# A 256-row attention trunk in fp32r on one core: plain rows for the weight parts, and products in four passes of sixteen groups of eight columns

## The chip, the cores and the metric

The kernel runs on one core of a Trainium2 chip. Its engines work side by side, each through its own list of instructions in order: TensorE (PE) multiplies, VectorE (DVE) and ScalarE (ACT) do the arithmetic on tiles, GpSimd (POOL) and SyncE (SP) mostly issue DMAs. The weight loads of TensorE are told apart as PEld. The metric is the device time in microseconds, the median of several runs. Fp32r is the 32-bit type in which the products are made; a number is given to them as the sum of two fp32r parts, a high and a low one.

## The reference

x has 256 rows of 4096 columns; there are 32 heads of 128, and only layer 0 runs (DEPTH is 1). Cut to what matters:

```python
h = x + attn_branch(rms_norm(x, norm_attn), w_in_attn, w_out_attn)
return rms_norm(h, final_norm)

def attn_branch(xn, w_in, w_out):            # w_in 4096 x 16384, w_out 4096 x 4096
    q, k, v, g = jnp.split(xn @ w_in, 4, axis=-1)
    o = stick_breaking_attention(to_heads(q), to_heads(k), to_heads(v))
    return (o * jax.nn.silu(g)) @ w_out

# per head, for s < t:  z = q.k / sqrt(128)
# log_a[t, s] = log_sigmoid(z_ts) + sum over s < j < t of log_sigmoid(-z_tj);   o_t = sum_s exp(log_a) v_s
```

Nearly all of the work is in the two big products, x times w_in and o times w_out.

## The kernel before

The products are cut into 20 units of 512 x 2 output columns: 16 for w_in (two heads each, with their q, k, v and gate) and 4 for w_out. Each unit goes through 16 steps of 256 rows of the weights. In the first unit of each matrix a step is eight products of 128 x 128 by 128 x 512. In the other units ten of the sixteen steps use a scheme with seven products in place of eight (sums and differences of weight blocks, and of blocks of x, stand for the blocks), the other six steps eight. The outputs of a unit collect in seven accumulators in PSUM (`acc`, the rings `b1` to `b7`) and are combined at the unit's end.

A weight block arrives by a DMA from SP into a `raw` tile; for the steps with seven products GpSimd adds another block on top by a second DMA. VectorE makes the further sums inside `raw` (`sums`, lines 411 to 432). Then `piece` (line 438) splits the block: ScalarE writes the high part `wh`, a copy rounded to fp32r, and VectorE the low part `wl`, the block minus `wh`. A part holds two 512-column operands (c = 0 and 1), each made of two halves of 256 columns (i = 0 and 1). Parts of only one operand lie in a smaller tile, of which one half serves as `wh` and the other as `wl`; in the trace both bear the name wh. Of x, and later of the attention's output, the stationary operands are split in the same way: `sh` and `sl` for x, `oh` and `ol` for the output (the `forms`).

`mm3` (line 797) is one product: three matmuls, high by high, high by low and low by high, into one accumulator. `mm3` is called for the big products only; the attention's matmuls (tiles tr, z and o, and neg_tri for the scan along the keys) are written out by themselves, read plain rows, and write plain rows.

In the kernel before, `by_runs` (line 434) lays the 1024 columns of a part in runs of four: sixteen columns in a row hold four of (c 0, i 0), four of (c 0, i 1), four of (c 1, i 0), four of (c 1, i 1), and so on. A product reads its operand in two passes, one for each half: 64 runs of four columns, each run sixteen columns (64 bytes) after the one before. The accumulator is written in one plain row.

The order of the instructions comes from `Plan` (line 108), which runs through the program as a simulation of its own while the program is being written out, with a cost for each instruction, and gives every engine the waiting work with the lowest key. The products' order is fixed (`order`, line 301); their cost is `PRODUCT`, three times `tensor_ns(512)`, and the keys of the other work are multiples of it. Where the attention's work, the splits and the sums fall between the products thus hangs on `tensor_ns` (line 104). `SPREAD` (line 58) says from which step on the forms of the attention's output are made for w_out: form s may start when step 12 + s, counted from the start of the last unit of w_in, is done (`later_than`, line 941). The number of buffers (7 for raw, 7 for wh, 5 for wl) limits how far the splits run ahead of the products.

Of the kernel before, what the change touches and what calls it, by code (L numbers as in the profile page):

```python
# [11 lines left out]
F32R = mybir.dt.float32r  # L12
# [7 lines left out]
P = 128  # L20
# [6 lines left out]
HG = CW // P  # L27
NB = D // CW
W = 2 * CW
NJ = D // W  # L30
KT = 2
NS = KC // KT
EPS = 1e-6

RUN = 4
WARM, IDLE = 10, 640


# [9 lines left out]
LOWS = 5  # L48
# [6 lines left out]
KEPT = 5  # L55
LAST_ORDER = (5, 4, 2, 3)

SPREAD = (12, 1.0)
HEADS_AHEAD = 0
SUMS_LATER = 2  # L60
H_LATER = 6
# [40 lines left out]


def tensor_ns(n):
    return 0.4167 * n + 12.4 if n > 128 else 109.0


class Plan:
# [135 lines left out]
def kernel(  # L244
# [14 lines left out]
    wp = ctx.enter_context(tc.tile_pool(name="weights", bufs=1))  # L259
# [10 lines left out]
    def minus(out_, full, part):  # L270
        nc.vector.tensor_tensor(out=out_, in0=full, in1=part.bitcast(F32), op=ALU.subtract)
# [30 lines left out]
    for b in LAST_ORDER:  # L302
        order += [(n, k) for n in kept for k, prod in enumerate(parts[n]["prods"]) if prod[0] == b]
    starts, ends, first, left, place_of = {}, {}, {}, {}, {}
    PRODUCT = 3 * tensor_ns(W)
    for g, (n, k) in enumerate(order):
        p = parts[n]
# [17 lines left out]
    def dve(emit, n, key=None, more=0, **kw):  # L325
        n = n if isinstance(n, tuple) else (n,)
        cost = sum(vector_ns(m) for m in n) + 122 * (len(n) - 1) + more
        return nc.work("vector", cost, emit, soon() if key is None else key, **kw)

    def act(emit, n, key=None, **kw):  # L330
        n = n if isinstance(n, tuple) else (n,)
        cost = sum(scalar_ns(m) for m in n) + 100 * (len(n) - 1)
        return nc.work("scalar", cost, emit, soon() if key is None else key, **kw)
# [4 lines left out]
    def ten(emit, *n):  # L338
        return nc.work("tensor", 40 + sum(tensor_ns(m) for m in n), emit, nc.here - 1e4, wait=400)
# [20 lines left out]
    raw, wh, wl = {}, {}, {}  # L360
# [44 lines left out]
    def low_done(n):  # L405
        lows_left[n] -= 1
        if not lows_left[n]:
            nc.tell(("lows", n))
            tile_done(*parts[n]["tile"])

    def sums(q):

        a, b, c, d = quad_parts[q]
        one, two = raw[q, 0], raw[q, 1]
        for k in range(2):
            tile_left[q, k] += 1

        def add(to, at_, f, g, key, op=ALU.add):
            return dve(
                lambda: nc.vector.tensor_tensor(out=to[:, :, at_, :], in0=f, in1=g, op=op), W,  # L420
                key - SUMS_AHEAD * 1e3, more=120 if op == ALU.subtract else 10,
            )

        yield nc.until(("lows", a), ("T3", q))
        yield add(one, 0, one[:, :, 0, :], two[:, :, 0, :], first[c], ALU.subtract)
        yield nc.until(("lows", b))
        yield add(two, 1, one[:, :, 0, :], two[:, :, 1, :], first[c])
        nc.tell(("sums", c))
        yield add(one, 1, one[:, :, 0, :], one[:, :, 1, :], first[d])
        nc.tell(("sums", d))  # L430
        for k in range(2):
            tile_done(q, k)

    def by_runs(t):

        return t.rearrange("p (h c i e) -> p c i h e", c=KT, i=HG, e=RUN)

    def piece(n, c, there):

        p = parts[n]  # L440
        yield nc.until(*there)
        full = raw[p["tile"]][:, :, p["place"], :][:, :, c, :].rearrange("p i c (h e) -> p c i h e", e=RUN)
        h = wh[n][:, c]
        size = (c.stop - c.start) * W
        key = first[n] - (AHEAD * 1e3 if p["seven"] and p["i"] < 2 else 0)
        yield act(lambda: nc.scalar.copy(h, full), size, key - 2.0 * 1e3)
        if p["size"] == KT:
            if c.start == 0:
                yield nc.take("wl")
                wl[n] = by_runs(wp.tile([P, KT * W], F32R, tag="wl", name=f"wl{n}", bufs=LOWS))  # L450
                nc.tell(("lowslot", n))
            else:
                yield nc.until(("lowslot", n))
        l = wl[n][:, c]
        if n == 0:
            yield nc.until(("sh", c.start))
        yield dve(lambda: minus(l, full, h), size, key, more=10)
        for k in range(c.start, c.stop):
            nc.tell(("low", n, k))
        low_done(n)  # L460

    def split(size, tag, bufs):
        for n, p in enumerate(parts):
            if p["size"] != size:
                continue
            q = p["quad"]
            t = p["tile"][1]
            if size == KT:
                yield nc.take(tag)
            yield nc.until(("raw", q, t))  # L470
            if size < KT:
                yield nc.take(tag)
            wh[n] = by_runs(wp.tile([P, KT * W], F32R, tag="wh" if size == KT else "s", name=f"wh{n}", bufs=bufs))
            if size == 1:
                wh[n], wl[n] = wh[n][:, 0:1], wh[n][:, 1:2]
            cuts = [slice(k, k + 1) for k in range(KT)] if n == 0 else [slice(0, size)]
            lows_left[n] = len(cuts)
            if p["seven"] and p["i"] == 0:
                nc.start(sums(q))
            for c in cuts:  # L480
                nc.start(piece(n, c, [("sums", n)] if p["seven"] and p["i"] > 1 else [("raw", q, t)]))
# [315 lines left out]
    def mm3(out_, a, b, start, stop):  # L797

        (ah, al), (bh, bl) = a, b
        if len(bh.shape) == 4:  # L800
            out_ = out_.rearrange("p (i h e) -> p i h e", i=HG, e=RUN)
        kw = dict(skip_group_check=True)
        nc.tensor.matmul(out_, ah, bh, start=start, stop=False, **kw)
        nc.tensor.matmul(out_, ah, bl, start=False, stop=False, **kw)
        nc.tensor.matmul(out_, al, bh, start=False, stop=stop, **kw)
# [135 lines left out]
    def later_than(u, s):  # L941
        s = int(SPREAD[0] + SPREAD[1] * s)
        return "used", u + s // NS, s % NS
# [284 lines left out]
    def product(n, k):  # L1228
        p = parts[n]
        b, f, c = p["prods"][k]  # L1230
        h, l = forms[p["s"]]
        mm3(
            ev[p["u"]][b],
            (h[:, PLACES[f], :], l[:, PLACES[f], :]),
            (wh[n][:, c], wl[n][:, c]),
            starts[p["u"], b] == (n, k),
            ends[p["u"], b] == (n, k),
        )

    def products():  # L1240
        for g, (n, k) in enumerate(order):
            p = parts[n]
            u, s = p["u"], p["s"]
            b, f, c = p["prods"][k]
            if u < 1:
                what = "s"
            elif u < OUT0:
                what = "n"
            elif u == OUT0:
                what = "o"  # L1250
            else:
                what = "r" if u == LAST and s in EIGHT_LAST else "p"
            if starts[u, b] == (n, k):
                yield nc.take(f"b{b}")
                ev.setdefault(u, {})[b] = acc.tile([P, W], F32, tag=f"b{b}", name=f"acc{u}_{b}")
            yield nc.until(("low", n, c), ("form", what, s), lead=nc.LEAD)
            yield nc.work(
                "tensor", PRODUCT, lambda: product(n, k), g * PRODUCT, after=lambda n=n, k=k: done(n, k), hold=False
            )
            nc.here = g * PRODUCT  # L1260

    together(split(KT, "w", HIGHS), split(1, "s", SINGLES), products(), x_stats(), x_factor(), constants())

    def in_turn(works):
# [55 lines left out]
```

## Time and profile before

| what | us |
|---|---|
| median of three runs (1722.3 to 1724.72) | 1723.66 |
| the profiled execution | 1725.08 |
| its span, first to last instruction | 1722.3 |
| TensorE busy in it | 1704.4 |
| VectorE busy in it | 1634.9 |
| ScalarE busy in it | 1199.3 |
| HBM read, 403.98 MB | 239 GB/s over the span |

A row of a group reads: line, engine, operation, tile written and tiles read, shape and count, then busy time in us, mean of one in ns, and idle time ahead of it with what ended that. Nearly every row has line 127, the planner's helper that emits all instructions; so groups are told apart by their tiles. A matmul lasts longer than the time to the next one's start, since they are pipelined. A row of windows reads: stretch, then for each engine busy us and count of instructions, the granted clock of TensorE, the DMAs' share and GB/s; of the engines the order is PE, PEld, DVE, ACT, POOL, and where one tile and engine were asked for, there is only one such pair. A row of waits reads: who waited for whom, us in total, times, longest. Where a row of a tile has three numbers after its count, they are the shortest, median and longest duration in ns.

### The profile page before, as it was taken

The page shows a single profiled execution, that of the slowest core. Times are in us where ns is not written, and L with a number is a line of the kernel's source. Part 1 is how long each engine was busy: PE and PEld are TensorE (multiplying, and loading weights), DVE is VectorE, ACT ScalarE, POOL GpSimd, SP SyncE. Part 2 cuts the span into 40 slices and gives each one's busy share as a digit, 9 for nine tenths or more (in the row PEclk, how much of TensorE's full clock was granted, in tenths as well). Part 3 has the DMA queues.
Part 4 walks back from the last instruction along what each step waited for, and adds up shares of the span by engine and source line. Part 5 has one row for each costly group of instructions (what it writes and reads, how often), then busy time and mean ns, then how long its engine had stood idle before and what let it go on. Part 6 is the DMA issues. An engine that isn't in the chain of part 4 may idle for free. (4 is left out here: it accounts for less than half of the span.)

```text
span 1722.3 us, 25298 instructions
## 1 busy us (share of the span) xinstructions
PE 1704.4 (99%) x7735; PEld 1415.7 (82%) x7735; DVE 1634.9 (95%) x2106; ACT 1199.3 (70%) x1640; POOL 335.6 (19%) x407
## 2 busy tenths in 40 slices
PE   9999999999999999999999999999999999999997
PEld 7888888888888888888888888888888888878786
DVE  8899999999999999999999999999999978999997
ACT  8986767676767676767676767676767765666655
POOL 0012222222222222121212121212222112122120
PEclk9999999999999999999999999999999999999999
DMA  9978787878787979797978787878788978898895
GB/s 342 329 199 234 220 248 221 247 215 259 206 264 197 266 194 273 191 270 199 266 202 257 207 249 216 245 214 245 221 238 224 278 243 253 232 258 248 242 301 196
DMA packets 249384, 413.82 MB, mean 240 GB/s; under 512 B 28128, under 2 KB 73440, under 8 KB 249248
## 3 DMA queue, kind: packets, MB, share of 16 engines
q1 hardware_dynamic: 194544, 354.24, 62.2%
q0 software_dynamic: 54416, 57.70, 20.4%
q8 instruction: 60, 0.98, 0.2%
q14 instruction: 76, 0.62, 0.1%
q10 hardware_dynamic: 288, 0.28, 0.0%
HBM read 403.98 MB, written 8.13 MB: 239 GB/s over the span
## 5 line engine op out<-in xcount | busy, mean ns | idle before, releaser
L127 ACT CAST wh<-raw 128x1024 fp32r<-128x1024 f32 (+1 forms) x995 | 922.3, 969 | 412.2 <-DVE raw L127 207.3
L127 DVE TENSOR_TENSOR wl<-raw,wh 128x1024 fp32r<-128x1024 f32 (+1 forms) x818 | 974.9, 1218 | 33.7 <-PE acc L127 13.5
L127 PE MATMUL acc<-wh,sh 128*128 128x512 f32 x2048 | 783.5, 394 | 1.1 <-DVE qk_sb L127 0.7
L127 PE MATMUL acc<-wh,sl 128*128 128x512 f32 x1898 | 733.3, 386 | 0.0
L127 PE MATMUL acc<-wl,sh 128*128 128x512 f32 x1748 | 675.3, 386 | 0.0
L127 POOL DMA_DIRECT2D raw<-in_w_in_dram x300 | 263.1, 996 | 977.8 <-DMA raw<-in_w_in_dram 326.5
L127 PEld LDWEIGHTS acc<-wh,sh 128*128 128x128 f32 x2048 | 384.1, 188 | 77.9 <-issue 2.2
L127 PEld LDWEIGHTS acc<-wh,sl 128*128 128x128 f32 x1898 | 356.1, 188 | 73.4 <-DVE sl L127 0.5
L127 PEld LDWEIGHTS acc<-wl,sh 128*128 128x128 f32 x1748 | 328.5, 188 | 61.5 <-DVE wl L127 0.4
L127 DVE TENSOR_TENSOR raw<-raw,raw 128x512 f32<-128x512 f32 x354 | 242.6, 685 | 12.8 <-DMA raw<-in_w_in_dram 9.7
L127 PE MATMUL acc<-wh,oh 128*128 128x512 f32 x512 | 194.5, 388 | 0.0
L127 PE MATMUL acc<-wh,ol 128*128 128x512 f32 x485 | 187.1, 386 | 0.0
L127 PE MATMUL acc<-wl,oh 128*128 128x512 f32 x458 | 177.4, 387 | 3.8 <-DVE wl L127 3.8
L127 DVE TENSOR_TENSOR wh<-raw,wh 128x512 fp32r<-128x512 f32 x177 | 121.2, 684 | 1.3 <-ACT wh L127 1.3
L127 DVE TENSOR_TENSOR raw<-raw 128x512 f32<-128x512 f32 x177 | 121.0, 683 | 0.0
L127 PEld LDWEIGHTS acc<-wh,oh 128*128 128x128 f32 x512 | 96.0, 188 | 19.5 <-ACT wh L127 0.4
L127 PEld LDWEIGHTS acc<-wh,ol 128*128 128x128 f32 x485 | 90.9, 187 | 18.4
L127 PEld LDWEIGHTS acc<-wl,oh 128*128 128x128 f32 x458 | 85.8, 187 | 23.3 <-DVE wl L127 6.6
L127 POOL DMA_DIRECT2D raw<-in_w_out_dram x54 | 47.3, 976 | 182.1 <-DMA raw<-in_w_out_dram 65.9
L127 ACT ACTIVATE f<-f 128x384 f32<-128x384 f32 x96 | 50.5, 526 | 3.0
L127 ACT CAST oh<-p 128x512 fp32r<-128x512 f32 (+3 forms) x46 | 20.8, 467 | 23.5 <-DVE p L127 16.7
L127 POOL DMA_DIRECT2D p<-spill x28 | 17.0, 682 | 85.3 <-ACT gl L127 26.8
(83 smaller groups left out, 781.8 us busy)
## 6 DMA issues: line engine op xcount, KB each, us to landing
raw<-in_w_in_dram SPq DMA_DIRECT2D x1024, 256.0 KB, 4.5
raw<-in_w_out_dram SPq DMA_DIRECT2D x256, 256.0 KB, 4.4
raw<-in_w_in_dram POOLq DMA_DIRECT2D x300, 128.0 KB, 5.2
p<-spill POOLq DMA_DIRECT2D x28, 256.0 KB, 4.8
raw<-in_w_out_dram POOLq DMA_DIRECT2D x54, 128.0 KB, 5.3
xr<-in_x_dram SPq DMA_DIRECT2D x16, 256.0 KB, 5.4
xres<-in_x_dram SPq DMA_DIRECT2D x16, 256.0 KB, 6.2
out_dram<-h SPq DMA_DIRECT2D x16, 256.0 KB, 2.8
```

The lines of the kernel that those rows point to most:

```text
L127: return self.tc.keep_in_program_order(getattr(self.engine, name)(*args, **kw))
```

## The change

A part now lies in plain rows: its 1024 columns are c 0 with both halves one after the other, then c 1. ScalarE and VectorE write it so. `mm3` rearranges the operand and the accumulator alike, in four passes: pass q reads columns 8q to 8q + 7 of each 32, that is sixteen groups of eight columns, each group 32 columns (128 bytes) after the one before; it writes the accumulator's columns of the same numbers. So the accumulator holds what it held before, at the same places, and is filled in another order. Beside this the planner's cost of a matmul of 512 columns falls from 225.75 to 221.85 ns, and the forms of the attention's output may start two steps sooner.

```diff
-RUN = 4
+RUN, ROUNDS = 8, 4
...
-SPREAD = (12, 1.0)
+SPREAD = (10, 1.0)
...
 def tensor_ns(n):
-    return 0.4167 * n + 12.4 if n > 128 else 109.0
+    return 0.4167 * n + 8.5 if n > 128 else 109.0
...
-    def by_runs(t):
-
-        return t.rearrange("p (h c i e) -> p c i h e", c=KT, i=HG, e=RUN)
+    def halves(t):
+
+        return t.rearrange("p (c i n) -> p c i n", c=KT, i=HG)
...
-        full = raw[p["tile"]][:, :, p["place"], :][:, :, c, :].rearrange("p i c (h e) -> p c i h e", e=RUN)
+        full = raw[p["tile"]][:, :, p["place"], :][:, :, c, :].rearrange("p i c n -> p c i n")
...
-                wl[n] = by_runs(wp.tile([P, KT * W], F32R, tag="wl", name=f"wl{n}", bufs=LOWS))
+                wl[n] = halves(wp.tile([P, KT * W], F32R, tag="wl", name=f"wl{n}", bufs=LOWS))
...
-            wh[n] = by_runs(wp.tile([P, KT * W], F32R, tag="wh" if size == KT else "s", name=f"wh{n}", bufs=bufs))
+            wh[n] = halves(wp.tile([P, KT * W], F32R, tag="wh" if size == KT else "s", name=f"wh{n}", bufs=bufs))
...
     def mm3(out_, a, b, start, stop):
         (ah, al), (bh, bl) = a, b
-        if len(bh.shape) == 4:
-            out_ = out_.rearrange("p (i h e) -> p i h e", i=HG, e=RUN)
+        in_rounds = lambda t: t.rearrange("p (h q e) -> p q h e", q=ROUNDS, e=RUN)
+        out_, bh, bl = (in_rounds(t) for t in (out_, bh, bl))
...
-            (wh[n][:, c], wl[n][:, c]),
+            tuple(t[:, c].rearrange("p i n -> p (i n)") for t in (wh[n], wl[n])),
```

The first products in TensorE's row, before and after (the number behind a tile's name is that of the buffer's turn, the shape that of the output as it is written):

```order
L127 MATMUL acc_1_142<-wh_155,sh_79 128x512
L127 MATMUL acc_1_142<-wl_161,sh_79 128x512
L127 MATMUL acc_1_142<-wh_155,sl_80 128x512
L127 MATMUL acc_6_197<-wh_155,sh_79 128x512
L127 MATMUL acc_6_197<-wl_161,sh_79 128x512
```

```order
L127 MATMUL acc_1_142<-wh_155,sh_79 128x4x16x8
L127 MATMUL acc_1_142<-wl_161,sh_79 128x4x16x8
L127 MATMUL acc_1_142<-wh_155,sl_80 128x4x16x8
L127 MATMUL acc_6_197<-wh_155,sh_79 128x4x16x8
L127 MATMUL acc_6_197<-wl_161,sh_79 128x4x16x8
```

The products keep their places; only the way through the columns is another. Between them the attention's matmuls stand a few products sooner or later.

VectorE's row at the end of the w_in stage, where the first form of the attention's output is made (`ol`, from the tile `p` that comes back from its spill), of before and of the change:

```order
L127 TENSOR_TENSOR raw_0_12831<-raw_0_12831,raw_1_12765 128x2x256
L127 TENSOR_TENSOR raw_1_12765<-raw_0_12831,raw_1_12765 128x2x256
L127 TENSOR_TENSOR wl_12932<-raw_0_12868,wh_12925 128x4x64x4
L127 TENSOR_TENSOR raw_0_12831<-raw_0_12831 128x2x256
L127 TENSOR_TENSOR wl_12946<-raw_1_12765,wh_12895 128x4x64x4
```

```order
L127 TENSOR_TENSOR raw_0_12835<-raw_0_12835,raw_1_12772 128x2x256
L127 TENSOR_TENSOR wl_12933<-raw_0_12871,wh_12927 128x1024
L127 TENSOR_TENSOR raw_1_12772<-raw_0_12835,raw_1_12772 128x2x256
L127 TENSOR_TENSOR ol_12942<-p_12894,oh_12941 128x512
L127 TENSOR_TENSOR raw_0_12835<-raw_0_12835 128x2x256
L127 TENSOR_TENSOR p_12894<-p_12894 128x2x128
L127 TENSOR_TENSOR wl_12962<-raw_1_12772,wh_12893 128x1024
```

In the row of before the first ol stands ten instructions further down; now it and the difference on p come ahead of the split of raw_1. The low parts are written as 1024 columns in a row where they were written in runs of four.

VectorE's row in the w_out stage, at the place where TensorE waits longest for a low part (about 1521 us; h is the residual's row, and the low part waited for is wl_14546 before, wl_14549 now):

```order
L127 TENSOR_TENSOR raw_1_14360<-raw_0_14390,raw_1_14360 128x2x256
L127 TENSOR_TENSOR h_1_14002<-h_1_14002,xres_1_14481 128x512
L127 TENSOR_TENSOR raw_0_14390<-raw_0_14390 128x2x256
L127 TENSOR_TENSOR wl_14523<-raw_1_14444,wh_14512 128x4x64x4
L127 TENSOR_TENSOR wl_14546<-raw_1_14360,wh_14455 128x4x64x4
```

```order
L127 TENSOR_TENSOR raw_1_14363<-raw_0_14390,raw_1_14363 128x2x256
L127 TENSOR_TENSOR h_1_14000<-h_1_14000,xres_1_14484 128x512
L127 TENSOR_TENSOR raw_0_14390<-raw_0_14390 128x2x256
L127 TENSOR_TENSOR wh_14517<-raw_1_14431,wh_14517 128x512
L127 TENSOR_TENSOR wl_14549<-raw_1_14363,wh_14451 128x1024
```

Only one instruction ahead of the low part has changed, a split of 1024 columns for one of 512; the sums and the residual's addition stay ahead of it.

## The prediction

> **What bounds the kernel now.** I read first the page's busy times, then the waits of TensorE, then the windows of the acc tiles and of all engines, and last the groups by shape.
>
> ```profile
> PE 1704.4 (99%) x7735; PEld 1415.7 (82%) x7735; DVE 1634.9 (95%) x2106; ACT 1199.3 (70%) x1640; POOL 335.6 (19%) x407
> PEclk9999999999999999999999999999999999999999
> ```
>
> The waits of TensorE, in us, times, and the longest:
>
> ```profile
> PE acc L127 <- DVE wl L127: 3.8, 3, 1.9
> PE warm L127 <- DVE idle L127: 1.3, 1, 1.3
> PE acc L127 <- DVE qk_sb L127: 0.7, 1, 0.7
> PE acc L127 <- ACT wh L127: 0.4, 1, 0.4
> PE tr L127 <- DVE gated L127: 0.2, 1, 0.2
> ```
>
> TensorE (PE) is busy for 99% of the span at its full granted clock, and all its waits on other engines together are 6.4 us (the five rows; three of them, 3.8 us, are for a low part wl that VectorE (DVE) had not written). So the span is the number of matmuls times the time from one start to the next, which I call the pitch. VectorE, at 95%, stands right behind.
>
> The product matmuls are six groups:
>
> ```profile
> L127 PE MATMUL acc<-wh,sh 128*128 128x512 f32 x2048 | 783.5, 394 | 1.1 <-DVE qk_sb L127 0.7 <-ACT wh L127 0.4
> L127 PE MATMUL acc<-wh,sl 128*128 128x512 f32 x1898 | 733.3, 386 | 0.0
> L127 PE MATMUL acc<-wl,sh 128*128 128x512 f32 x1748 | 675.3, 386 | 0.0
> L127 PE MATMUL acc<-wh,oh 128*128 128x512 f32 x512 | 194.5, 388 | 0.0
> L127 PE MATMUL acc<-wh,ol 128*128 128x512 f32 x485 | 187.1, 386 | 0.0
> L127 PE MATMUL acc<-wl,oh 128*128 128x512 f32 x458 | 177.4, 387 | 3.8 <-DVE wl L127 3.8
> ```
>
> The windows of the acc tiles give the pitch where nothing but products runs:
>
> ```profile
> 1430.00:1500.00 70.00, 70.00 (x312) 1.00 0.83 244
> 1606.00:1660.00 54.00, 54.00 (x241) 1.00 0.87 266
> ```
>
> Each matmul of about 0.386 us overlaps the next, so 312 starts fill 70.39 us and 241 fill 54.39 us: a pitch of 225.6 and 225.7 ns. The groups add up to 7149 matmuls; times 225.7 ns that is 1613.5 us of the 1722.3. One nanosecond of pitch is worth 7.1 us.
>
> **The change, part by part.** 1. *The read and the write of each product in four passes.* Nothing in the trace has this pattern, so its pitch has to be bounded. What the trace does have is the same kind of operand (fp32r) read in plain rows, in the scan of the attention:
>
> ```profile
> 804.98 0.34 PE L127 MATMUL z<-fh,neg_tri 128*128 128x384 f32 x1
> 805.16 0.34 PE L127 MATMUL z<-fl,neg_tri 128*128 128x384 f32 x1
> 805.33 0.22 PE L127 MATMUL z<-fh,neg_tri 128*128 128x128 f32 x1
> 805.39 0.27 PE L127 MATMUL z<-fl,neg_tri 128*128 128x128 f32 x1
> ```
>
> Two matmuls of 384 columns take 805.33 - 804.98 = 0.35 us, 0.175 each; one of 128 takes 0.06. The 256 columns between are 0.115 us, 0.45 ns a column, so 512 plain columns would take 0.175 + 128 x 0.45 = 232 to 233 ns. This is the upper bound. Today's products, read in two passes of runs of four columns, take 225.7: hopping is not punished there, it is some 7 ns better than plain reading. The lower bound is what the quickest of today's products show:
>
> ```profile
> L127 PE MATMUL acc<-wl,sh x1748: 378/385/795, 6.8 to 1370.7; 128*128 128x512 f32 x195
> ```
>
> The shortest lasts 378 ns where the median lasts 385 and the mean 386; 7 to 8 ns off the pitch make 218, and I take this as a pitch with nothing lost. Over that floor one pass loses about 14.5 ns and two passes 7.7, so the doubled number of passes roughly halved the loss. A further doubling would leave about 4: 222 ns. The runs are longer too, eight columns for four, which by the plain row should work the other way, and the accumulator is now written in the same order, which no row shows; the ends 218 and 232 stay for the range. I take 222, since it lies nearest to the measured 225.7 on the side to which more passes point. The saving is 3.7 ns x 7149 = 26.5 us if TensorE is never kept waiting.
>
> Here a rule of the Trainium skill speaks against the change. The page PSUM — Partial Sum Buffer, section Specifications (TRN2), says of lines of 8 bytes that "any non-contiguous AP slows matmuls significantly". The page gives no figure, and before the change every accumulator is written in one row, so the trace cannot agree or differ; Advanced Engine Details and Errata, section Memory Cachelines, softens it: it asks only for every two consecutive elements to be contiguous, which runs of eight are. By the first rule the time would be that of the dear write among the rivals, by the second nothing is lost; the sum goes by the rows.
>
> 2. *The weight parts in plain rows.* The writers of wh and wl now write rows instead of runs of four. The trace has both kinds of write at equal size:
>
> ```profile
> L127 DVE TENSOR_TENSOR raw<-raw,raw 128x512 f32<-128x512 f32 x354 | 242.6, 685 | 12.8 <-DMA raw<-in_w_in_dram 9.7 <-DMA raw<-in_w_out_dram 0.8
> L127 DVE TENSOR_TENSOR wh<-raw,wh 128x512 fp32r<-128x512 f32 x177 | 121.2, 684 | 1.3 <-ACT wh L127 1.3
> L127 ACT CAST wh<-raw 128x512 fp32r<-128x512 f32 x179 | 109.0, 619 | 71.5 <-PE acc L127 51.9 <-DMA raw<-in_w_in_dram 9.5 <-DMA raw<-in_w_out_dram 4.2
> L127 ACT CAST sh<-xs 128x512 fp32r<-128x512 f32 x15 | 9.3, 621 | 0.5
> ```
>
> Rows 685, runs 684 on VectorE; runs 619, rows 621 on ScalarE (ACT). Between -1 and +2 ns on some 2000 instructions is at most 2 us of engine time; I cost it at nothing. It is hidden while TensorE leads; if VectorE led, the bound of 1 ns x 995 writes would be 1 us on the end.
>
> 3. *The planner's cost and SPREAD.* 8.5 for 12.4 and 10 for 12 move only the order. No instruction, DMA or byte is added on any queue; SP and POOL issue the same loads, a handful of them one or two places apart. The forms of the attention's output come two steps earlier, the first of them ten rows sooner in VectorE's order. The room for them is VectorE's lull around 1400 us (18.26 us busy of 25 in a row of the next fence). I cost the order at nothing, between -2 and +2 us, the size of the longest wait for wl today (1.9).
>
> 4. *What is late next.* TensorE gaining 3.7 of 225.7 is 1.6%, so VectorE must do in 196.8 us what it now does in 200:
>
> ```profile
> 500.00:700.00 200.00, 200.00 (x917) 166.88 (x917) 193.85 (x237) 142.45 (x188) 42.36 (x50) 1.00 0.81 231
> 700.00:900.00 200.00, 200.00 (x926) 167.32 (x925) 194.87 (x242) 143.34 (x191) 42.89 (x50) 1.00 0.82 230
> ...
> 1400.00:1425.00 25.00, 25.00 (x115) 20.88 (x115) 18.26 (x30) 15.96 (x26) 2.67 (x5) 1.00 0.72 234
> ...
> 1500.00:1525.00 25.00, 23.08 (x99) 18.07 (x98) 24.32 (x30) 16.83 (x24) 5.24 (x6) 1.00 0.94 268
> 1525.00:1550.00 25.00, 25.00 (x113) 20.79 (x112) 24.98 (x32) 14.03 (x17) 5.26 (x6) 1.00 0.86 248
> 1550.00:1575.00 25.00, 24.44 (x109) 20.03 (x108) 24.56 (x29) 16.14 (x21) 4.94 (x6) 1.00 0.84 240
> 1575.00:1600.00 25.00, 24.98 (x111) 20.47 (x111) 24.79 (x30) 13.71 (x19) 5.60 (x7) 1.00 0.95 280
> 1600.00:1625.00 25.00, 23.68 (x106) 19.39 (x105) 23.83 (x29) 17.06 (x25) 4.62 (x6) 1.00 0.88 251
> ```
>
> In the w_in stage it is busy 193.9 to 194.9 of 200 (the third busy figure of a row), so 196.8 still holds it, at 99%. Part of its idle time today is that it has run ahead as far as the buffers let it:
>
> ```profile
> DVE wl L127 <- PE acc L127: 13.5, 25, 1.8
> ```
>
> (its 25 waits for a buffer that a product still reads), and this part goes away by itself. In the w_out stage after 1500 us there is no such room: VectorE is busy 122.5 of the 125 us shown, and TensorE already loses 3.8 us there. What TensorE gains after about 1440 us is therefore mostly spent waiting for wl.
>
> **The sum.** The product matmuls from 1440 us on are
>
> ```profile
> L127 PE MATMUL acc<-wh,oh 128*128 128x512 f32 x403 | 151.4, 386 | 0.0
> L127 PE MATMUL acc<-wh,ol 128*128 128x512 f32 x376 | 144.9, 385 | 0.0
> L127 PE MATMUL acc<-wl,oh 128*128 128x512 f32 x349 | 135.4, 388 | 3.8 <-DVE wl L127 3.8
> ```
>
> 1128 up to 1700 us, so 6021 lie elsewhere: 6021 x 3.7 ns = 22.3 us, kept whole. The 1128 could give 4.2 us; between none and all of it, I keep half, 2. The span falls by 24.3 us, from 1722.3 to 1698.0. The profiled execution's own time is 1725.08, 2.8 us more than its span and 1.4 us above the median of the runs, 1723.66; against the median I forecast 1723.66 - 24.3 = 1699.4, so 1699 us.
>
> **The rivals.** *VectorE takes over.* If its idle time of 5 to 6 us in 200 were forced by what it waits for and stayed, it could not work faster at all and the whole gain would turn into waits for wl. For it speaks the 99% above, against it the 13.5 us of waits for buffers and ScalarE's and the loads' lower shares (143 of 200; 0.82). With half of the w_in gain lost the time is 1723.7 - 11 = 1712; the case runs from 1706 to 1720.
>
> *The dear write: it costs more in passes than the read saves.* The place is the accumulator's bank: 64 runs for each matmul where there was one. Today's read has 128 runs and loses at most 7.7 ns by them, 0.06 ns a run; an accumulating write touches its bank twice, so let a run cost 0.12 ns: 64 of them are 7.7 ns on 222, a pitch of 229.7, and 4.0 x 7149 = 29 us more: 1752. It decides from 3.7 / 64 = 0.058 ns a run. This is what the skill's PSUM rule above would do here. Against it: the plain scan also writes its bank in one row and is slower per column than today's products, so the loss that the trace shows sits with the read.
>
> *The pattern doesn't matter at all.* The plain scan may be slow for another reason, its short length say; then the pitch stays at 225.7 and only the order differs: 1724, within 3 us.
>
> *All of the loss goes.* Then the pitch is 218 and TensorE would need 55 us less, but VectorE's 1634.9 us of busy work is in the way; with half of its idle time of 87.4 us kept, the time is about 1680.
>
> **How the numbers follow.** The forecast has 0.64 (its own range 1691 to 1706), VectorE taking over 0.13, no effect 0.06, the dear write 0.10, the full gain 0.07. The likeliest gives 1699. Leaving out the dear write and half of the full gain, and the upper part of the case without effect, gives 1684 to 1720. What this kernel can tell from no change is about 0.2%, 3.4 us, so: faster 0.64 + 0.12 + 0.07 + 0.01 = 0.84, the same 0.05 (most of the case without effect and the end of VectorE's), slower 0.11.
>
> **What would show it.** Right: the windows of the acc tiles give a pitch of 221 to 223 ns everywhere, the mean of a product matmul falls from 386 to about 382, VectorE's share rises to 96 to 97%, its wl still lasts 1218, and PE's waits for wl grow from 3.8 to some 6 to 8 us, all in the w_out stage. Wrong: a pitch of 225 or more; or the pitch at 222 and waits for wl over 12 us, some of them before 1440 us; or a pitch under 220 and TensorE's share well under 98%.

## The result, and the profile after

The changed kernel takes 1753.64 us (median of four runs, 1751.32 to 1757.16) against 1724.19 us before: slower by the ratio 1.0174, 95% interval 1.0154 to 1.0194. The profiled execution has a span of 1753.0 us, 30.7 us more than the 1722.3 before.

The page's rows that answer to those of before, then the waits of TensorE:

```profile
PE 1734.8 (99%) x7735; PEld 1420.3 (81%) x7735; DVE 1634.7 (93%) x2106; ACT 1206.0 (69%) x1640; POOL 335.4 (19%) x407
...
L127 DVE TENSOR_TENSOR wl<-raw,wh 128x1024 fp32r<-128x1024 f32 (+1 forms) x818 | 974.1, 1216 | 45.7 <-PE acc L127 19.7
L127 PE MATMUL acc<-wh,sh 128*128 128x512 f32 x2048 | 794.6, 400 | 1.6 <-DVE qk_sb L127 1.5
L127 PE MATMUL acc<-wh,sl 128*128 128x512 f32 x1898 | 744.1, 392 | 1.3 <-DVE sl L127 1.3
L127 PE MATMUL acc<-wl,sh 128*128 128x512 f32 x1748 | 685.0, 392 | 0.0
```

```profile
PE tr L127 <- DVE gated L127: 1.8, 1, 1.8
PE acc L127 <- DVE qk_sb L127: 1.5, 3, 0.9
PE acc L127 <- DVE sl L127: 1.3, 1, 1.3
PE warm L127 <- DVE idle L127: 1.3, 1, 1.3
```

TensorE is still what bounds the kernel, and waits no longer than before (5.9 us against 6.4). VectorE has the same work in the same time (1634.7 us, the low parts 1216 ns each) and more room, 93%. A product matmul lasts 5 or 6 ns longer (394 to 400 ns in the first of these groups). The windows of the acc tiles in the first unit, where no attention lies between the products, before and after, give the pitch:

```profile
30.00:90.00 60.00, 60.00 (x268) 1.00 0.98 325
```

```profile
30.00:90.00 60.00, 60.00 (x262) 1.00 0.93 316
```

60.39 us over 268 and 262 starts: 225.3 and 230.5 ns. Over the whole trace I take as the pitch the mean of the times from one product's start to the next product's, without those over 260 ns, which hold a wait or the first matmul behind the attention's (some 6800 of 6988 remain; for the one kernel below with a pitch over 260 the limit is 600): 225.66 ns before and 230.08 after. 4.42 ns x 7149 = 31.6 us is the whole loss, to within 1 us. So by its size alone the loss looks like one cause, the four passes. The runs show that it is not.

### The profile page after: what moved, and what is told of

Read it like the earlier page. It is cut to its first block, busy times and chain, and to the rows that moved or that the text cites. A ratio compares the mean times of both kernels' runs of the same rounds, so it can differ in the third digit from the quotient of the medians.

```text
span 1753.0 us, 25252 instructions
## 1 busy us (share of the span) xinstructions
PE 1734.8 (99%) x7735; PEld 1420.3 (81%) x7735; DVE 1634.7 (93%) x2106; ACT 1206.0 (69%) x1640; POOL 335.4 (19%) x407
## 4 chain that ended last, share of the span: by engine, by line
PE 94%; DMA 2%; DVE 2%; issue 1%; ACT 0%; SPq 0%; DVEq 0%; ACTq 0%; POOLq 0%
PE acc L127 89%; PE z L127 2%; PE o L127 2%; DMA raw<-in_w_in_dram 1%; PE tr L127 1%; DMA raw<-in_w_out_dram 1%; DVE wl L127 1%; DMA p<-spill 0%; DVE raw L127 0%; DVE h L127 0%; ACT wh L127 0%; DVE qk_sb L127 0%; DVE gv_sb L127 0%; SPq L127 0%; DVE scalars L127 0%
## 5 line engine op out<-in xcount | busy, mean ns | idle before, releaser
L127 DVE TENSOR_TENSOR wl<-raw,wh 128x1024 fp32r<-128x1024 f32 (+1 forms) x818 | 974.1, 1216 | 45.7 <-PE acc L127 19.7
L127 PE MATMUL acc<-wh,sh 128*128 128x512 f32 x2048 | 794.6, 400 | 1.6 <-DVE qk_sb L127 1.5
L127 PE MATMUL acc<-wh,sl 128*128 128x512 f32 x1898 | 744.1, 392 | 1.3 <-DVE sl L127 1.3
L127 PE MATMUL acc<-wl,sh 128*128 128x512 f32 x1748 | 685.0, 392 | 0.0
L127 DVE TENSOR_TENSOR raw<-raw,raw 128x512 f32<-128x512 f32 x354 | 242.4, 685 | 34.2 <-DMA raw<-in_w_in_dram 31.9
L127 DVE SCALAR_TENSOR_TENSOR gv_sb<-acc,scalars,gv_sb 128x512 f32<-128x512 f32 x45 | 33.4, 742 | 0.0
```

Of the source, the lines that this page charges most:

```text
L127: return self.tc.keep_in_program_order(getattr(self.engine, name)(*args, **kw))
```

## The experiments

Each kernel ran once with a profile, own_cost in three more rounds. Spans are those of the profile; before has 1722.3, and its times beside these runs were 1719.0 us (beside `plain`, `read4`, `write4` and `order_only`) to 1726.7, so a difference under 4 us says nothing. All pitches are the means just defined.

### The read or the write

From the changed kernel, mm3 alone is edited. In `plain` both rearrangements go. In `read4` the accumulator is written in one row and only the operand is read in passes; in `write4` it is the other way round (in both, and in `write_run2` below, the outputs' columns come out permuted, and the work is the same):

```diff
 # read4
-        out_, bh, bl = (in_rounds(t) for t in (out_, bh, bl))
+        bh, bl = (in_rounds(t) for t in (bh, bl))
+        out_ = out_.rearrange("p (q h e) -> p q h e", q=ROUNDS, e=RUN)
 # write4
-        out_, bh, bl = (in_rounds(t) for t in (out_, bh, bl))
+        out_ = in_rounds(out_)
+        bh, bl = (t.rearrange("p (q h e) -> p q h e", q=ROUNDS, e=RUN) for t in (bh, bl))
```

> The changed kernel with the four passes taken out of mm3: operand and accumulator both go through in one plain row; all else stays. Two theories of the 4.4 ns that the four passes cost (pitch 230.1 after, 225.7 before). Theory W, the write: the stepped write of the accumulator costs some 8 ns and the stepped read saves some 4; then a plain row of both has the 232 ns worked out from the scan, span about 1753 + 1.9 x 7.15 = 1767 us. Theory R, the read: the longer runs of eight read worse than runs of four, and the write is free; then plain also gives about 232, 1767 us. A pitch under 228 would speak against both, since then the plain row was never slow.

> Only the read goes in four passes; the accumulator is written in one plain row, so the columns of each accumulator come out in another order, and everything behind them works on permuted columns. Theory W: 222 ns, span about 1753 - 8 x 7.15 = 1696 us (a little more if VectorE holds it up). Theory R: 230 ns, 1753 us.

> Only the write goes in four passes; the operand is read in one plain row (the accumulators' columns come out permuted, as in the other run with one side alone). Theory W: the plain read's 232 and 8 ns for the write, 240 ns, span about 1824 us. Theory R: as the plain row, 232 ns, 1767 us.

| pitch in ns (span in us) | written in four passes | written in one row |
|---|---|---|
| read in four passes | 230.08 (after, 1753.0) | 230.07 (`read4`, 1754.6) |
| read in one row | 227.27 (`write4`, 1748.4) | 227.30 (`plain`, 1741.4) |

The first unit's windows of `read4`, `write4` and `plain`:

```profile
30.00:90.00 60.00, 60.00 (x261) 1.00 0.92 316
```

```profile
30.00:90.00 60.00, 60.00 (x266) 1.00 0.93 322
```

```profile
30.00:90.00 60.00, 60.00 (x266) 1.00 0.94 321
```

The order in which the accumulator is written costs nothing: 0.0 ns, in both rows of the table. Theory W, that the write costs the time, falls, and with it the dear write of the forecast. Of theory R the first half holds: what the pitch loses lies in the read. Its second half does not: a plain row has 227.3 ns, not 232. The Trainium skill's rule of the page PSUM — Partial Sum Buffer (Specifications (TRN2)), that a non-contiguous pattern slows matmuls significantly, does not show for runs of eight columns.

The spans of `plain` and `write4` are too long for their pitch, though, by 7 and 14 us: 1.64 x 7.149 = 11.7 us over before would be 1734. The 7 us between these two do not lie in the pitch but in gaps: those over 430 ns between products sum to 13.2 us in `plain` and 18.8 in `write4`. Where the gaps come from, the next kernels say.

### The order

```diff
 # order_only: the kernel before with
-SPREAD = (12, 1.0)
+SPREAD = (10, 1.0)
-    return 0.4167 * n + 12.4 if n > 128 else 109.0
+    return 0.4167 * n + 8.5 if n > 128 else 109.0
 # cost_only: the second of the two alone
```

> The kernel before with the planner's two numbers of the change (8.5 and 10) alone: layout, read and write as before. Both theories: the pitch stays at 225.7 and the span within 2 us of 1722. If the order has a share in the loss, the waits of TensorE for wl or the span show it: more than 1725 us.

> The kernel before with 8.5 for 12.4 in the planner's cost alone (SPREAD stays 12). With both numbers the kernel before took 1742.2 us at a pitch of 225.5. If the cost does it, since the planner then puts VectorE's work where inputs are not yet there: 1738 to 1744 us with waits all through the w_in stage. If SPREAD does it: 1720 to 1725 us.

`order_only` has before's pitch, 225.5, and a span of 1742.2 us; `cost_only` 1745.3. So the planner's cost by itself, with the same read, costs some 20 us, and SPREAD adds nothing to it. I had priced the order at nothing. The two losses do not lie at the same places, though. The last product of w_in starts 20.5 us later than before in `order_only` and 14.9 us later in `cost_only`, which then loses 8 us more behind it, 4.8 of them in one wait for the high part of the attention's output:

```profile
PE acc L127 <- ACT oh L127: 5.1, 2, 4.8
```

`order_only`, whose forms may start two steps sooner, has no such wait. So SPREAD seems to move a loss rather than to do nothing; the net of 3 us is within the noise of single runs. The waits of TensorE for VectorE, and of VectorE for loads, in `order_only`:

```profile
PE acc L127 <- DVE qk_sb L127: 12.1, 11, 1.9
PE acc L127 <- DVE wl L127: 2.6, 3, 1.2
```

```profile
DVE raw L127 <- DMA raw<-in_w_in_dram: 44.4, 26, 3.2
```

and the latter before:

```profile
DVE raw L127 <- DMA raw<-in_w_in_dram: 9.7, 9, 2.4
```

VectorE's row now has, once or twice in most units, a sum over a block that has not landed. VectorE waits (44 us in all), everything behind it in its row comes later, and among that is the addition that frees an accumulator (qk_sb). It is not that more work stands ahead of it: ahead of the first such addition of the last unit of w_in VectorE has 1658 instructions and 1428.5 us of work before and 1660 and 1427.2 us in `order_only`, but its waits for loads up to there have grown from 10.4 to 44.8 us. TensorE then stands before that accumulator's next product. Behind the first 20 us, its times over 430 ns between products sum to 18.7 us beyond the pitch, against 5.4 before. One such place in `order_only`: VectorE's two waits for loads ahead of a unit's end, by time, and then TensorE at that end:

```profile
665.11 0.69 DVE L127 TENSOR_TENSOR raw<-raw,raw 128x512 f32<-128x512 f32 x1 [2.81 <-DMA raw<-in_w_in_dram]
682.69 0.69 DVE L127 TENSOR_TENSOR raw<-raw,raw 128x512 f32<-128x512 f32 x1 [2.58 <-DMA raw<-in_w_in_dram]
```

```profile
698.62 0.39 PE L127 MATMUL acc<-wh,sl 128*128 128x512 f32 x1
700.92 0.50 PE L127 MATMUL acc<-wh,sh 128*128 128x512 f32 x1 [1.91 <-DVE qk_sb L127]
...
703.33 0.63 PE L127 MATMUL acc<-wh,sh 128*128 128x512 f32 x1
703.76 0.63 PE L127 MATMUL acc<-wl,sh 128*128 128x512 f32 x1
704.18 0.63 PE L127 MATMUL acc<-wh,sl 128*128 128x512 f32 x1
```

Beside these two waits VectorE is idle for only 0.33 us up to the unit's end, so it can't make them up. The gap is 2.3 us from start to start, and after it the pitch is 0.43 us for a time. The windows of that stretch (PE alone, then the granted clock):

```profile
700.00:704.00 4.00, 3.08 (x12) 0.78 0.82 125
704.00:708.00 4.00, 4.00 (x16) 0.79 0.56 188
```

The granted clock falls to 0.78 in these windows. So a wait of some two microseconds can be followed by a stretch at half the pace: 11 product matmuls of this kind in `order_only`, 2.2 us.

Is it that the cost is too low, or would any other order than that of before do this? And what is the read's share with the order of before?

```diff
 # cost_high: the kernel before with
-    return 0.4167 * n + 12.4 if n > 128 else 109.0
+    return 0.4167 * n + 16.7 if n > 128 else 109.0
 # read_alone: the changed kernel with 12.4 and SPREAD (12, 1.0); plain_old_order: plain with the same
 # own_cost: the changed kernel with
-    return 0.4167 * n + 8.5 if n > 128 else 109.0
+    return 0.4167 * n + 16.7 if n > 128 else 109.0
```

> The kernel before with 16.7 in place of 12.4 in the planner's cost, which then takes TensorE for slower (230 ns) than it is (225.7). With 8.5 (222 ns) the kernel took 1745.3 us, 23 us more. Theory optimism: only a cost below the true pitch hurts, since VectorE's row then holds work whose inputs are not there yet and which the accumulators' release stands behind; here 1720 to 1727 us. Theory any change: the order of before happens to fit and another is worse either way; over 1730 us.

> The changed kernel with the planner's two numbers of before (12.4 and 12); layout, read and write as changed, so every engine has the order of before. Theory P, the pattern makes the loss: pitch 230.1, the waits of before, span 1722.3 + 4.4 x 7.149 = 1754 us, at most some 4 us less since TensorE is slower and VectorE has more room. Theory O, the order makes part of the loss: under 1748 us.

> Plain rows in the read and the write, with the order of before. Its pitch in the new order was 227.3, its span 1741.4 us, which is 7 us more than 1722.3 + 1.64 x 7.149 = 1734.0. Theory O: in the order of before those 7 us go, 1733 to 1735 us, and VectorE's waits for loads fall from 33 us to some 10. Theory P: they stay, since they belong to the plain layout, 1741 us.

> The changed kernel, SPREAD 10 and all, with one number changed: the planner's cost is 16.7, which gives 230.05 ns for a matmul of 512 columns, the pitch that the changed kernel has. Theory two causes: what the order costs goes (11 us between the change at 1753.0 and the same read in the order of before at 1742.0), and what the read costs stays: pitch 229 to 230, 1738 to 1746 us, slower than before by 0.8 to 1.3%. If the 11 us came from SPREAD, or from chance in the quick and slow stretches of the pitch: 1748 to 1755 us.

| kernel | read | planner's pitch | pitch | span | VectorE's waits for loads of w_in |
|---|---|---|---|---|---|
| before | runs of four, two passes | 225.8 | 225.66 | 1722.3 | 9.7 |
| `order_only` | same | 221.9 | 225.52 | 1742.2 | 44.4 |
| `cost_only` | same | 221.9 | 225.56 | 1745.3 | 37.8 |
| `cost_high` | same | 230.1 | 225.64 | 1722.3 | 3.3 |
| `plain` | one row | 221.9 | 227.30 | 1741.4 | 33.0 |
| `plain_old_order` | one row | 225.8 | 227.20 | 1733.7 | 3.5 |
| after | runs of eight, four passes | 221.9 | 230.08 | 1753.0 | 31.9 |
| `read_alone` | same | 225.8 | 228.88 | 1742.0 | 1.0 |
| `own_cost` | same | 230.1 | 229.39 | 1744.3 | 0 |

`cost_high` is as fast as before with a cost about as far off on the other side. A planner that took TensorE for slower than it is did no harm here; one that took it for faster did, and the waits for loads go with it: 32 to 44 us in the rows with 221.9, under 10 in the others. `plain_old_order` confirms it: 1733.7, where 1733.3 follows from its own pitch, and its waits for loads are 3.5 us. `read_alone` goes to theory O by its span: the same read takes 1742.0 us in the order of before, 11 us less than in its own. Neither theory had the way it came about, a lower pitch (228.88). `own_cost` takes 1748.13 us in the median (ratio to before 1.0138, 1.0121 to 1.0155), so with a cost near the true pitch 5.5 us of the median come back and 8.7 of the profiled span; the two intervals just touch (1.0154 and 1.0155). Its profiled span, 1744.3, lies in the range that I gave for the order, its median time just inside the one for chance, so this kernel alone does not tell the two apart.

Those 9 to 11 us are no waits: behind the first 20 us, TensorE's times over 430 ns between products sum to 2.7 us beyond the pitch after, 3.9 in `read_alone` and 3.1 in `own_cost`. Most come from the pitch, 230.08 against 228.88 (8.6 us) and 229.39 (5.0 us), with the same pattern of read. The windows of the acc tiles in the first unit, 20 to 90 us, after and in `read_alone`, show how:

```profile
20.00:90.00 70.00, 70.00 (x305) 1.00 0.95 326
```

```profile
20.00:90.00 70.00, 70.00 (x320) 1.00 0.98 339
```

70.39 us over 305 and over 320 starts, 230.8 and 220.0 ns: the same products in the same row of TensorE, through the whole stretch. With this read the pitch has two levels, and keeps one until something interrupts the products, an attention matmul or a wait; most stretches fall on the slow one. Over the whole traces, in stretches of at least six products, the quick ones have a mean of 220 to 221 ns and all others one of 230.6. The quick ones hold 285 products after, 281 in `read4` (the same order and read), 706 in `own_cost` and 1138 in `read_alone`, of some 6700 each. At 10.4 ns a product, `own_cost` and `read_alone` gain 4.4 and 8.9 us over after by this, close to the 5.0 and 8.6 of the pitch. But a few long stretches hold much of it: one of 417 products at 1445 us in `own_cost`, two of 373 and 235 in `read_alone`. That the order shifts which stretches are quick is thus seen; that a better cost makes more of them quick is not shown by one order each. What decides the level stays open: by the trace the weight load of the next matmul starts 2 to 3 ns after the matmul's start on both levels.

### Which property of the read

All of these have plain rows, the order of before and another (RUN, ROUNDS) in mm3, as

```diff
-RUN, ROUNDS = 8, 4
+RUN, ROUNDS = 4, 4
```

> Plain rows, order of before, but four passes of 32 groups of four columns, each 16 columns (64 bytes) after the one before: run and hop of the kernel before, passes and rows of the change. If the run's length or the hop makes the pitch: 225.7 as in before, span 1722 us. If the number of passes makes it: 230 ns, 1754 us. If it is the plain row that the weights lie in (512 columns in 2 KB instead of 4 KB): between 227 and 230.

> Plain rows, order of before, read in eight passes of runs of four columns, 32 columns (128 bytes) from run to run: the hop of the change with the run of before. Runs of four at a hop of 16 columns gave 226.0 ns, runs of eight at a hop of 32 gave 228.9 (230.1 in the new order), in two kinds of stretches, of 220 and of 230 to 231. Theory hop: the hop of 128 bytes makes those two kinds, so they are here too, mean 228 to 231, span 1739 to 1755 us. Theory run: the run of four makes 226, span 1722 to 1726.

> Plain rows, order of before, two passes of runs of eight columns, 16 columns (64 bytes) from run to run: the run of the change with the hop of before. Theory hop: 226 ns, 1722 to 1726 us. Theory run: 228 to 231 ns with the two kinds of stretches, 1739 to 1755 us. Neither: near the plain row's 227.2, 1734.

> Plain rows, order of before, two passes of runs of sixteen columns, 32 columns (128 bytes) from run to run: half of each 128 bytes is passed over, as in run8_hop16, with both lengths doubled. Theory hop: as the change, 228 to 231 ns. Theory run: the longer the run the nearer to the plain row, 227 to 228 ns, 1733 to 1740 us.

> Plain rows, order of before, four passes of 64 groups of two columns, 8 columns from group to group. Measured so far: a quarter of each hop read (4 of 16, 8 of 32) 226.0 and 228.9 ns, a half (8 of 16, 16 of 32) 232.4 and 239.9, an eighth (4 of 32) 246.5. Theory quarter: what counts is that a pass reads a quarter of the row, that is four passes; here 220 to 230. Theory run within it: the shorter the run the quicker, under 226, span 1700 to 1722 us.

> The same with groups of sixteen of each 64 columns. Theory quarter: 220 to 230 ns. Theory run within it: over 229, towards 232 or more, span over 1745 us.

> The same with groups of 64 of each 256 columns, two groups in a pass. Theory quarter: 220 to 230 ns. Theory run within it: the order is nearly the plain row's by now, so 227 to 232 ns, span 1733 to 1768 us.

| kernel | columns in a run | from run to run | passes | pitch, ns | span, us |
|---|---|---|---|---|---|
| `run2_round4` | 2 | 8 | 4 | 461 | 3387.9 |
| before (row of 4 KB) | 4 | 16 | 2 | 225.66 | 1722.3 |
| `run4_round4` | 4 | 16 | 4 | 225.97 | 1723.4 |
| `run4_hop32` | 4 | 32 | 8 | 246.48 | 1862.7 |
| `run8_hop16` | 8 | 16 | 2 | 232.44 | 1764.5 |
| `read_alone` | 8 | 32 | 4 | 228.88 | 1742.0 |
| `run16_hop32` | 16 | 32 | 2 | 239.94 | 1816.9 |
| `run16_round4` | 16 | 64 | 4 | 239.35 | 1812.4 |
| `run64_round4` | 64 | 256 | 4 | 227.21 | 1731.0 |
| `plain_old_order` | 512 | | 1 | 227.20 | 1733.7 |

No single property orders this table. The theories of the hop and of the run both fall: none of `run4_hop32`, `run8_hop16` and `run16_hop32` came out in the range of either. Of the passes, two give 225.7, 232.4 and 239.9 ns, four give 226.0 to 239.4 and 461; of the runs, four give 226 and 246; of the hops, 32 gives 229, 240 and 246. Of the five that read a quarter of the row in a pass, three are quick (226.0, 228.9, 227.2), but sixteen of 64 (239.35) is not, and two of eight is far out: the theory of the quarter falls, and that of the run within it with it, since four is quicker than two and 64 quicker than 16. What can be said: stepping helps a plain row by at most 1.5 ns (four of sixteen), costs up to 19 ns in the other patterns of four columns or more, and groups of two columns, 8 bytes, double the time. No pattern tried beats before; the rule behind the table stays open. A mean of the table can also hide levels: in `run4_round4`, stretches of twelve products run from 223 to 228 ns, where the plain row's are nearly all at 227.

The groups of two were the last question: is it their read or their write?

```diff
 # write_run2: write4 in the order of before, with
-RUN, ROUNDS = 8, 4
+RUN, ROUNDS = 2, 4
```

> Order of before, operand read in one plain row, the accumulator written in four passes of 64 groups of two columns (its columns come out permuted, as in the runs with one side alone). Read and write together in groups of two took 460 ns. If the write of so short runs does it: 460 ns, about 3380 us. If the read does: 227.2 ns as the plain row, 1731 to 1735 us.

The rows of the low part's product in `write_run2` and in `run2_round4`:

```profile
L127 PE MATMUL acc<-wl,sh 128*128 128x512 f32 x1748 | 681.0, 390 | 0.2 <-DVE wl L127 0.2
```

```profile
L127 PE MATMUL acc<-wl,sh 128*128 128x512 f32 x1748 | 1146.1, 656 | 0.0
```

Written in groups of two, read plain, a matmul lasts 390 ns and the pitch is 227.21, the plain row's; the span is 1733.7. So the doubling lies with the read too, and the accumulator took pairs of columns, 8 bytes, in this stepped order for nothing.

## Why the prediction was wrong

The direction was wrong: 1699 forecast with 0.84 for faster, 1753.6 measured, outside the range of 1684 to 1720.

**What bounds the kernel** held: TensorE's pitch times 7149, before and after, and one ns is 7.1 us.

**The step that failed first** is the upper bound, "512 plain columns would take 0.175 + 128 x 0.45 = 232 to 233 ns". A plain row takes 227.2. The slope came from two matmuls of 128 columns, of which the first starts 0.06 us ahead of the second, but the second 0.11 us ahead of the next product (805.39 to 805.50 in the trace of before, a row that I left out). 0.06 is no pitch of a steady stream. The other bound, 218, came from the duration of the shortest matmul, and a duration is no pitch: no twelve products in a row in any run come closer than 219.8 ns on average. With 227.2, passes save 1.5 ns at before's pattern and not 7, and nothing is left to extrapolate.

**The step that followed from it**, "the doubled number of passes roughly halved the loss. A further doubling would leave about 4: 222 ns", is wrong in kind: the number of passes has no such effect (226.0, 228.9 and 239.4 ns with four of them). Of 222 ns, 228.9 to 230.1 came, 26.5 us of gain became 23.0 to 31.6 of loss. I had two points and a change that moved three things at once, the run, the hop and the passes; I should have kept the bounds and given "slower" half of the chance.

**The write** I left inside the bounds; it measured 0.0 ns. The rival of the dear write ended at 1752 us, 2 us from the result, by luck: its 0.12 ns for each run of the write came to nothing, for 64 runs (`write4`) and for 256 (`write_run2`); the loss lies in the read and the order. The section Memory Cachelines of the Trainium skill's Advanced Engine Details and Errata, which I took to soften the rule, also states it, one line ahead of the sentence on pairs; of the two, only the sentence on pairs agrees with these runs.

**The weight parts in plain rows**, costed at nothing, held: 1216 ns for the low part after, 1218 before.

**The order**, "I cost the order at nothing, between -2 and +2 us", failed too. At before's pitch it costs 20 us (`order_only`), on the path that I had named for VectorE taking over, but by another mechanism: not too much work, since the same amount of it stands ahead of the additions, but work in the wrong place, behind loads that had not landed. At the slower pitch that came, VectorE still waits 31.9 us for loads, but TensorE only 5.9 us in all, and the order's part is 9 to 11 us, most of it through the share of quick and slow stretches. With this order the kernels of 225.5 to 227.3 ns (`order_only`, `plain`, `write4`) took 1741 to 1748 us. What it would have cost at 222 ns no run shows: there the planner's cost, 221.85, would have been the true pitch.

**What is late next** was right as far as it went, that VectorE has no room for a faster TensorE; that the planner's cost was itself below the true pitch, and so made an order for a TensorE that isn't there, I did not see, because I counted instructions that moved and not what they would stand behind.

The parts of the loss, from the runs: `read_alone` against before 19.7 us (23.0 from the pitch, 3 back since the gaps over 260 ns between products add less beyond it, 22.5 us against 25.6), and after against `read_alone` 11.0 us (8.6 from the pitch, 2 from the stretches of attention, which the order spreads differently). These are differences of single runs, each good to some 4 us.

## What to carry to other kernels

Take a pitch only from a long stretch of the same instruction; a short burst's first gap says nothing, and one unlike row is not a trend. Where a kernel is ordered by a planner, a cost below what the trace shows is a change of its own: try it alone, and let it err on the slow side (here `cost_high` lost nothing, `cost_only` 23 us). And when two edits are bundled, a loss that one of them explains to the microsecond may still be the sum of two.

## What the runs showed of the hardware

The order in which a matmul writes its accumulator was free in the two stepped orders tried, groups of eight and groups of two columns (8 bytes): 227.27 and 227.21 ns against 227.30 and 227.20 in one row.

The order in which it reads its moving operand in fp32r was not: 226 to 246 ns for 512 columns with runs of four and more, and 461 with runs of two, with no simple law. The pitch of one pattern can have two levels, 220.0 and 230.8 ns in the first unit, that last for hundreds of matmuls.

A short gap can cost TensorE its clock. Of the twelve gaps of 2.1 to 2.4 us between two products' starts in all these runs, six were followed by 3.4 us at a granted clock of 0.5, with starts 0.43 us apart: two of the four in `order_only`, both in `write4`, one each in `plain_old_order` and `write_run2`. The other six, one of them in the kernel before, were not. A gap of 5.0 us in `cost_only` was followed by 10.2 us of it. The Trainium skill's page TensorE: Matmul & The Clock Gate (Part 1: The HAM clock gate) puts the fall after an idle window of some 3.4 us that runs freely; here gaps shorter than that were enough in six cases of twelve.
